# A two-layer decoder on one core: token tile 0's next-stage input made during tile 1's last matmuls, and no modulation sums in a stage's last blocks

## The chip, the core and the metric

One core of a Trainium2 chip runs the whole program in one launch. The metric is the device time of one execution in microseconds (us). Times quoted from a trace are those of one profiled execution, counted from its first instruction.

## The reference

Two decoder layers act on x, 256 tokens of width 2048, float32. Each layer has a token mixer and an MLP, each fed by a modulated input and closed by a LayerNorm:

```
mod = silu(c) @ w_ada[l] + b_ada[l]
sh_a, sc_a, g_a, sh_m, sc_m, g_m = split(mod, 6)
h = x * (1 + sc_a) + sh_a
y = mixer(h)                        # projections, 8 + 8 heads, output projection w_o
x = layernorm(ALPHA * x + (1 + g_a) * y)
h = x * (1 + sc_m) + sh_m
y = square(relu(h @ w_up)) @ w_down  # hidden 8192
x = layernorm(ALPHA * x + (1 + g_m) * y)
```

## The kernel before

The tokens are two tiles of 128. Every weight is read as float32 in **blocks** of 256 rows by 512 columns (two k-tiles of 128 rows, 512 KB, a DMA of line 140 into one of 7 buffers `raw`). ScalarE (ACT) rounds the block to `wh` (line 134), VectorE (DVE) makes the remainder `wl = raw - wh` (line 135), and TensorE (PE) forms each product from three matmuls: hi·wh, hi·wl, lo·wh (lines 302 to 304 for `proj`, token-major; 328 to 331 for `proj_T`; 908 and 910 for the MLP's `up`). `wh` and `wl` have three buffers each, so a block can be split at most three blocks ahead of PE.

The modulation `c @ w_ada` is not done on PE. It is made of **sums** on DVE, one per 512 KB of `w_ada` (line 148, the data loaded by line 156 into the same 7 buffers). Their order is a list `side`: `block()` advances it by a rate per block (`RATES`), and `side_until` advances it at once as far as somebody needs a result. Sixteen sums give one part of the modulation; its accumulator is then transposed on PE (line 166) and reduced on DVE (line 171).

There are four stages: mixer and MLP of layer 0, mixer and MLP of layer 1, so three inner **boundaries**. The mixer ends with the output projection of 4 chunks of 512 columns (8 blocks each); after a chunk `add_gated` multiplies the result by the gate, adds it to `xacc` and takes statistics (lines 496, 497, 499 for each tile). In the last chunk of a stage `proj_tail` holds the last 4 blocks in SBUF (buffers `room`), runs them for token tile 0 and then for token tile 1, and calls `norm_first` on tile 0: statistics, a power on GpSimd (POOL, line 507), four normalizations (line 512). After the tail `norm_h` does the same for tile 1 and `make_h` builds the next stage's input `hT`: transposes on PE (line 471), scale and shift on ACT (line 484), rounding and remainder on DVE (lines 486, 487). The first blocks of the next stage take both tiles at once.

A scheduler in the framework sets the order in which each engine gets its instructions; an engine then runs its own list in that order.

Of the kernel before, what the change touches and what calls it, by code (L numbers as in the profile page):

```python
# [18 lines left out]
P = 128  # L19
# [30 lines left out]
SKIP = 2  # L50
AHEAD = 10
TAIL = (8, 12)
OTAIL = 8
# [7 lines left out]
STEP = ((2, 2), (2, 2))  # L61
RATES = ((0.8, 0.8, 1.0, 0.6, 1.2), (1.1, 0.53, 0.64, 0.25))

# [10 lines left out]
def decoder(ctx: ExitStack, tc: tile.TileContext, x, c, positions, w_ada, b_ada, w_in, b_f,  # L74
# [230 lines left out]

    def proj(po, lhs, wrows, c0, kt0, kt1, first=True, last=True):
# [10 lines left out]
    def proj_T(po, hT, wrows, c0, kt0, kt1, first=True, last=True):  # L317
# [16 lines left out]
    def proj_tail(po, lhs, wrows, c0, kt0, kt1, done):  # L334


        room = big.tile([P, 4, 2, 2, CW], F32R, tag="hT", name="room")
# [175 lines left out]

    def norm_first(stats):

        ms = row_stats(stats, 0)
        for q in range(4):
            normalize(0, q, *ms)

    def norm_h(stats, A, B, coef, key, end=KT):  # L520

        ms = [None] + [row_stats(stats, t) for t in range(1, NT)]
        hT = big.tile([P, KT, 2, S], F32R, tag="hT", name="hT")

        def steps():
            for q in range(4):
                for t in range(1, NT):
                    normalize(t, q, *ms[t])
                yield from make_h(hT, A, B, q * 4, q * 4 + 4, coef)

        h_steps[:] = [steps(), 0, end]
        hold[0] = HOLDS[key]
        need_h(AHEAD)
        return hT
# [220 lines left out]

    def mixer(l, hT, gate_key, stats, passes, done):

# [22 lines left out]
        def chunk(name, kt0=None, kt1=None, hold=False):  # L780
# [6 lines left out]
            if name in ("fq0", "fk0", "fq1", "fk1"):  # L787
                proj_T(po, hT, wr, c0, kt0, kt1, fresh, not hold)
            else:
                proj(po, lhs, wr, c0, kt0, kt1, fresh, not hold)  # L790
            if hold:
# [88 lines left out]
        for chs in ((0, 1), (2,), (3,)):  # L880
            pos = [[mm() for _ in range(NT)] for _ in chs]
            final_ch = chs == (3,)
            for kt0 in (8, 0):
                if kt0 == 0:
# [4 lines left out]
            if final_ch:  # L889
                proj_tail(pos[0], lhs_o, wo, 3 * CW, 8 - OTAIL, 8, lambda t: finish(3, pos[0], t))  # L890
# [4 lines left out]
    def mlp(l, hT, gate_key, stats, done, halves, pieces):  # L895

        wu = rows_of(w_up[l])

        def up(c0, kt0, kt1):
            pu = [mm(), mm(), bank(), bank()]  # L900
            for kb in range(kt0, kt1, 2):
                wh, wl = block(wu(kb, 2, c0, CW), 2, CW)
                need_h(kb + AHEAD)
                for j in range(2):
                    kt = kb + j
                    for f in range(4):
                        cs = slice(f * P, (f + 1) * P)
                        nc.tensor.matmul(pu[f], lhsT=wh[:, j, cs], rhs=hT[:, kt].rearrange("p a s -> p (a s)"),  # L908
                                         start=kt == kt0, stop=False)
# [4 lines left out]
        def up_narrow(c0, kt0, kt1):  # L914

            pu = [mm() for _ in range(2)]
            proj_T(pu, hT, wu, c0, kt0, kt1)
            return [p.rearrange("p (f s) -> p f s", f=2) for p in pu]
# [20 lines left out]
        for g in range(NG):  # L939
            Hs = [big.tile([P, 8, 2, S], F32R, tag="hm", name="Hs", bufs=2) for _ in range(2)]  # L940
            sets = range(GRP // CW)
            if g == 0 and halves is not None:
                for fs in range(LEAD):
                    part = g4([P, 4, S], "part")
                    for i, p in enumerate(up_narrow(fs * CW, 0, 8)):
                        nc.scalar.copy(part[:, 2 * i:2 * i + 2, :], p)
# [43 lines left out]
    def coeffs(l, vec, ln):  # L990
# [59 lines left out]
    for l in range(DEPTH):  # L1050
# [53 lines left out]
```

## Time and profile before

| | |
|---|---|
| median of 3 runs | 2377.34 us (2375.9 to 2378.76) |
| the profiled execution | 2369.32 us |
| its span, first to last instruction | 2367.6 us |
| PE busy | 2281.3 us (96%) |
| DVE busy | 1790.1 us (76%) |
| ACT busy | 1155.3 us (49%) |
| DMA read | 615.07 MB, 261 GB/s over the span |

PE is busy for all but some 86 us of the span, so time can come only from its idle stretches or from its work; DVE's share is an average, near full in the first half of the program and lower in the second.

### The profile page before, as it was taken

What the parts mean: (1) busy time and instruction counts of PE and PEld (TensorE: products, weight loads), DVE (VectorE), ACT (ScalarE), POOL (GpSimd) and SP (SyncE); (2) the same over time, 40 slices, a digit from 0 to 9 for tenths busy, and PEclk for the clock granted to TensorE, in tenths of its full rate; (3) what the DMA queues carried; (4) which work ended last, traced back from release to release, by engine and by line L of the source; (5) the groups of instructions that cost most, each with busy time, mean ns of one, the idle gap of its engine ahead of it and who ended that gap; (6) DMA issues with size and microseconds to landing.
All of it is one profiled execution on the core that took longest, in us unless ns stands there. A gap on an engine that the chain in (4) does not pass through costs nothing.

```text
span 2367.6 us, 33293 instructions
## 1 busy us (share of the span) xinstructions
PE 2281.3 (96%) x12444; PEld 1959.6 (83%) x12444; DVE 1790.1 (76%) x2339; ACT 1155.3 (49%) x1684; POOL 35.1 (1%) x60
## 2 busy tenths in 40 slices
PE   4999999899999999999999999999999999999998
PEld 3878798699989888888777778987888888888886
DVE  7899888988888778888777975667675666555657
ACT  2543675344546345346444663444554553553542
POOL 0000010000000000000000000000000000000000
PEclk9999999999999999999999999999999999999999
DMA  9999688889898888888759877765777777756653
GB/s 344 326 331 308 193 265 305 312 315 325 303 349 301 302 281 309 312 293 300 273 186 303 292 226 234 233 215 170 221 263 251 229 242 240 230 189 195 187 188 123
DMA packets 309890, 619.37 MB, mean 262 GB/s; under 512 B 24200, under 2 KB 25048, under 8 KB 309728
## 3 DMA queue, kind: packets, MB, share of 16 engines
q1 hardware_dynamic: 309728, 617.25, 77.6%
q8 instruction: 97, 1.59, 0.3%
q14 instruction: 65, 0.53, 0.1%
HBM read 615.07 MB, written 2.10 MB: 261 GB/s over the span
## 4 chain that ended last, share of the span: by engine, by line
PE 76%; DVE 9%; DMA 9%; issue 3%; ACT 2%; POOL 0%; SPq 0%; DVEq 0%; ACTq 0%; POOLq 0%
PE mm L303 13%; PE mm L302 13%; PE mm L304 13%; PE mm L908 7%; PE bank L908 7%; DMA rawa<-in_w_ada_dram 5%; PE mm L331 4%; PE mm L330 4%; PE mm L328 4%; PE mm L910 4%; PE bank L910 4%; DVE wl L135 4%; DVE acc L148 2%; DMA raw<-in_w_in_dram 1%; ACT wh L134 1%
## 5 line engine op out<-in xcount | busy, mean ns | idle before, releaser
L134 ACT CAST wh<-raw 128x1024 fp32r<-128x1024 f32 x752 | 789.5, 1052 | 929.5 <-PE mm L304 491.5
L135 DVE TENSOR_TENSOR wl<-raw,wh 128x1024 fp32r<-128x1024 f32 x752 | 913.7, 1221 | 347.2 <-ACT wh L134 343.9
L148 DVE SCALAR_TENSOR_TENSOR acc<-rawa,cact,acc 128x1024 f32<-128x1024 f32 x368 | 471.0, 1280 | 137.8 <-DMA rawa<-in_w_ada_dram 136.5
L303 PE MATMUL mm<-wl,Hs 128*128 128x512 f32 x992 | 386.5, 390 | 2.0 <-DVE wl L135 1.9
L302 PE MATMUL mm<-wh,Hs 128*128 128x512 f32 x992 | 386.2, 389 | 0.0
L304 PE MATMUL mm<-wh,Hs 128*128 128x512 f32 x992 | 386.0, 389 | 0.0
L331 PE MATMUL mm<-hT,wl 128*128 128x256 f32 x1024 | 289.6, 285 | 6.0 <-DVE wl L135 5.4
L328 PE MATMUL mm<-hT,wh 128*128 128x256 f32 x1024 | 290.9, 285 | 1.9 <-DVE hT L486 1.1
L330 PE MATMUL mm<-hT,wh 128*128 128x256 f32 x1024 | 289.8, 284 | 0.2 <-DVE hT L487 0.2
L908 PE MATMUL mm<-hT,wh 128*128 128x512 f32 x768 | 286.7, 396 | 0.5 <-DVE hT L487 0.5
L908 PE MATMUL bank<-hT,wh 128*128 128x512 f32 x768 | 286.2, 395 | 0.0
L303 PEld LDWEIGHTS mm<-wl,Hs 128*128 128x128 f32 x992 | 186.2, 188 | 41.9 <-DVE wl L135 3.5
L302 PEld LDWEIGHTS mm<-wh,Hs 128*128 128x128 f32 x992 | 186.2, 188 | 38.7
L304 PEld LDWEIGHTS mm<-wh,Hs 128*128 128x128 f32 x992 | 186.2, 188 | 38.6
L910 PE MATMUL mm<-hT,wl 128*128 128x256 f32 x768 | 215.5, 281 | 0.2 <-DVE wl L135 0.2
L910 PE MATMUL bank<-hT,wl 128*128 128x256 f32 x768 | 215.3, 280 | 0.0
L302 PE MATMUL mm<-wh,hT 128*128 128x512 f32 x512 | 200.8, 400 | 5.9 <-DVE hT L486 5.7
L303 PE MATMUL mm<-wl,hT 128*128 128x512 f32 x512 | 203.4, 397 | 3.1 <-DVE wl L135 2.7
L331 PEld LDWEIGHTS mm<-hT,wl 128*128 128x128 f32 x1024 | 196.0, 192 | 8.7 <-DVE wl L135 8.3
L304 PE MATMUL mm<-wh,hT 128*128 128x512 f32 x512 | 200.9, 393 | 0.0
L328 PEld LDWEIGHTS mm<-hT,wh 128*128 128x128 f32 x1024 | 196.8, 192 | 3.4 <-DVE hT L486 1.3
L330 PEld LDWEIGHTS mm<-hT,wh 128*128 128x128 f32 x1024 | 197.1, 192 | 0.8 <-DVE hT L487 0.4
(248 smaller groups left out, 2665.7 us busy)
## 6 DMA issues: line engine op xcount, KB each, us to landing
rawa<-in_w_ada_dram SPq DMA_DIRECT2D x384, 512.0 KB, 5.5
raw<-in_w_up_dram SPq DMA_DIRECT2D x256, 512.0 KB, 4.8
raw<-in_w_down_dram SPq DMA_DIRECT2D x256, 512.0 KB, 5.1
raw<-in_w_in_dram SPq DMA_DIRECT2D x192, 512.0 KB, 5.4
raw<-in_w_o_dram SPq DMA_DIRECT2D x64, 512.0 KB, 4.6
gb<-in_ln_g_dram SPq DMA_DIRECT2D x12, 256.0 KB, 5.5
bb<-in_ln_b_dram SPq DMA_DIRECT2D x12, 256.0 KB, 5.3
xacc<-in_x_dram SPq DMA_DIRECT2D x8, 256.0 KB, 6.7
```

Source lines behind the costliest of these rows:

```text
L134: nc.scalar.copy(wh, raw)
L135: nc.vector.tensor_sub(wl, raw, wh.bitcast(F32))
L148: nc.vector.scalar_tensor_tensor(acc, raw, k, acc, ALU.mult, ALU.add)
L302: nc.tensor.matmul(o, lhsT=hi, rhs=wh, start=start, stop=False)
L303: nc.tensor.matmul(o, lhsT=hi, rhs=wl, start=False, stop=False)
L304: nc.tensor.matmul(o, lhsT=lo, rhs=wh, start=False, stop=stop)
L328: nc.tensor.matmul(o, lhsT=wh[:, j, cs], rhs=hT[:, kt, 0, :], start=first and kt == kt0 and f % 2 == 0, stop=False)
L330: nc.tensor.matmul(o, lhsT=wh[:, j, cs], rhs=hT[:, kt, 1, :], start=False, stop=False)
L331: nc.tensor.matmul(o, lhsT=wl[:, j, cs], rhs=hT[:, kt, 0, :], start=False, stop=last and kt == kt1 - 1 and f % 2 == 1)
L908: nc.tensor.matmul(pu[f], lhsT=wh[:, j, cs], rhs=hT[:, kt].rearrange("p a s -> p (a s)"), start=kt == kt0, stop=False)
L910: nc.tensor.matmul(pu[f][:, 0:S], lhsT=wl[:, j, cs], rhs=hT[:, kt, 0, :], start=False, stop=kt == kt1 - 1)
```

## The change

1. **The list of sums.** In the tail's blocks the list is not advanced (`quiet=True`). The rate in layer 0's output projection goes from 1.0 to 1.2 sums a block. Before the last chunk of a stage, `ahead()` calls `side_until` for the modulation that the next stage's input needs; in layer 0's mixer these are the first two of four parts.
2. **Tile 0's input early.** `norm_first` allocates `hT` and, for the first 8 of 16 k-tiles, makes tile 0's part with `h_part`: 8 transposes, 8 activations 128 wide, rounding on ACT, remainder on DVE. `norm_h` does tile 1 in the same way; the other 8 k-tiles go through `make_h` for both tiles.
3. **The next stage's first three blocks** (6 k-tiles) are split together and run for tile 0, then for tile 1 (`lead`). In `proj` (boundary 2) the matmuls stay as they are, in another order. In `proj_T` (boundary 1) 72 matmuls 256 columns wide become 144 of 128 columns. In `up` (boundary 3) 24 of 512 become 48 of 256, and 24 of 256 become 48 of 128.
4. **The tail's buffers.** Two of the tail's four blocks stay in the `wh`/`wl` buffers, two go to a buffer of the tag `hm`, since `hT`'s is now taken.

```diff
-RATES = ((0.8, 0.8, 1.0, 0.6, 1.2), (1.1, 0.53, 0.64, 0.25))
+RATES = ((0.8, 0.8, 1.2, 0.6, 1.2), (1.1, 0.53, 0.64, 0.25))
...
-            ws.append(block(wrows(kb, 2, c0, CW), 2, CW, (room[:, i, 0], room[:, i, 1]) if i < 4 else None))
+            ws.append(block(wrows(kb, 2, c0, CW), 2, CW, into[i], quiet=True))
...
+    def h_part(hT, A, B, t, q):
+        ts = slice(t * P, (t + 1) * P)
+        pt = bank().rearrange("p (a s) -> p a s", a=4)
+        h32 = e2([P, 4, P], "h32")
+        for j in range(4):
+            kt = q * 4 + j
+            nc.tensor.transpose(pt[:, j, :], xacc[:, t, kt * P:(kt + 1) * P], ident)
+            nc.scalar.activation(h32[:, j, :], pt[:, j, :], AF.Identity, bias=B[:, kt:kt + 1], scale=A[:, kt:kt + 1])
+        hi = hT[:, q * 4:q * 4 + 4, 0, ts]
+        if t == 0:
+            nc.scalar.copy(hi, h32)
+        else:
+            nc.vector.tensor_copy(hi, h32)
+        nc.vector.tensor_sub(hT[:, q * 4:q * 4 + 4, 1, ts], h32, hi.bitcast(F32))
...
         for q in range(4):
             normalize(0, q, *ms)
+            if q < 2:
+                h_part(hT, A, B, 0, q)
...
+        if lead:
+            ws = lead_blocks(wrows, c0, kt0)
+            for t in range(NT):
+                for i in range(ONE):
...
+            if final_ch:
+                ahead()
...
+        def coefs_ahead(end=KT):
+            for k0 in range(0, end, 4):
+                cs[2](k0)
```

How this moves the instructions is read from the two programs' lists. First DVE in layer 0's output projection, from a block of the third chunk to the next splits. `L135` (later `L136`) is a split, `L148` (`L149`) a sum, `L496`, `L497`, `L499` (`L532`, `L533`, `L535`) are the third chunk's gate, addition and statistics. Before:

```order
L135 TENSOR_TENSOR wl_4410<-raw_4407,wh_4409 128x1024
L148 SCALAR_TENSOR_TENSOR acc_4313<-rawa_4404,cact_82,acc_4313 128x1024
L135 TENSOR_TENSOR wl_4441<-raw_4438,wh_4440 128x1024
L148 SCALAR_TENSOR_TENSOR acc_4313<-rawa_4435,cact_82,acc_4313 128x1024
L135 TENSOR_TENSOR wl_4462<-raw_4459,wh_4461 128x1024
L496 TENSOR_TENSOR tmp_4425<-mm_4238,gate0_2_1_3814 128x512
L496 TENSOR_TENSOR tmp_4429<-mm_4239,gate0_2_1_3814 128x512
L497 TENSOR_TENSOR xacc_84<-xacc_84,tmp_4425 128x512
L497 TENSOR_TENSOR xacc_84<-xacc_84,tmp_4429 128x512
L499 BN_STATS stats_103<-xacc_84 128x6 x2
L148 SCALAR_TENSOR_TENSOR acc_4313<-rawa_4456,cact_82,acc_4313 128x1024
L135 TENSOR_TENSOR wl_4483<-raw_4480,wh_4482 128x1024
```

Here `wl_4410` is the third chunk's last block, and two blocks of the last chunk (`wl_4441`, `wl_4462`) are split ahead of the third chunk's gate. After (the third chunk's last block is the split just above these rows):

```order
L149 SCALAR_TENSOR_TENSOR acc<-rawa,cact,acc 128x1024 x2
L532 TENSOR_TENSOR tmp<-mm,gate_2_1_3777 128x512
L149 SCALAR_TENSOR_TENSOR acc<-rawa,cact,acc 128x1024
L533 TENSOR_TENSOR xacc<-xacc,tmp 128x512
L532 TENSOR_TENSOR tmp<-mm,gate_2_1_3777 128x512
L535 BN_STATS stats<-xacc 128x6
L533 TENSOR_TENSOR xacc<-xacc,tmp 128x512
L149 SCALAR_TENSOR_TENSOR acc<-rawa,cact,acc 128x1024
L535 BN_STATS stats<-xacc 128x6
L149 SCALAR_TENSOR_TENSOR acc<-rawa,cact,acc 128x1024 x2
L136 TENSOR_TENSOR wl<-raw,wh 128x1024
```

No block of the last chunk is split ahead any more, and four sums stand between the third chunk's gate and the first split. PE at the same place, after (`mm_4264` is the third chunk, `mm_4450` the last one):

```order
L305 MATMUL mm_4264<-wh_4426,MXf_2949 128x512
L167 MATMUL bank_4473<-ident_75,acc_4225 128x128 x4
L167 MATMUL bank_4478<-ident_75,acc_4225 128x128 x4
L303 MATMUL mm_4450<-wh_4498,MXd_2163 128x512
L304 MATMUL mm_4450<-wl_4499,MXd_2163 128x512
```

The 8 transposes of the finished accumulator, which waits for the last of those sums, now stand ahead of the last chunk's first matmul; before they stood behind the tail. Last, DVE at boundary 3 after the change, from tile 0's gate on (`L541` leads to POOL's power, `L548` normalizes, `L564` is the remainder of tile 0's input):

```order
L532 TENSOR_TENSOR tmp<-mm,gate_2_1_11216 128x512
L533 TENSOR_TENSOR xacc<-xacc,tmp 128x512
L535 BN_STATS stats<-xacc 128x6
L539 BN_AGGR mv<-stats 128x2
L541 TENSOR_SCALAR ve<-mv 128x1
L136 TENSOR_TENSOR wl<-raw,wh 128x1024
L548 TENSOR_SCALAR xacc<-xacc,mv,rs 128x512 x4
L136 TENSOR_TENSOR wl<-raw,wh 128x1024
L532 TENSOR_TENSOR tmp<-mm,gate_2_1_11216 128x512
L533 TENSOR_TENSOR xacc<-xacc,tmp 128x512
L535 BN_STATS stats<-xacc 128x6
L564 TENSOR_TENSOR hT<-h_15715,hT 128x4x128
```

Two splits of the next stage's blocks, and tile 1's gate, addition and statistics, stand ahead of tile 0's remainder. Boundary 2 has the same order; boundary 1 has it too, with a sum behind tile 1's gate and another behind its statistics.

## Rows read from the trace of the kernel before

**Rows 1.** PE's waits, whole run: who, for whom, total us, times, longest us.

```profile
PE bank L471 <- DVE xacc L512: 15.0, 4, 6.9
```

**Rows 2.** PE timeline, layer 0's last output chunk: start us, us, instruction, count [idle].

```profile
441.10 0.39 PE L302 MATMUL mm<-wh,MXd 128*128 128x512 f32 x1
441.33 0.39 PE L303 MATMUL mm<-wl,MXd 128*128 128x512 f32 x1
...
446.54 0.61 PE L302 MATMUL mm<-wh,MXd 128*128 128x512 f32 x2
448.86 0.50 PE L303 MATMUL mm<-wl,MXd 128*128 128x512 f32 x1 [1.71 <-DVE wl L135]
```

**Rows 3.** DVE timeline, the same place.

```profile
442.81 1.28 DVE L496 TENSOR_TENSOR tmp<-mm,gate 128x512 f32<-128x512 f32 x2
444.00 1.29 DVE L497 TENSOR_TENSOR xacc<-xacc,tmp 128x512 f32<-128x512 f32 x2
445.21 1.28 DVE L499 BATCH_NORM_STATS2 stats<-xacc 128x6 f32<-128x512 f32 x2
446.40 1.27 DVE L148 SCALAR_TENSOR_TENSOR acc<-rawa,cact,acc 128x1024 f32<-128x1024 f32 x1
447.59 1.22 DVE L135 TENSOR_TENSOR wl<-raw,wh 128x1024 fp32r<-128x1024 f32 x1
448.72 1.28 DVE L148 SCALAR_TENSOR_TENSOR acc<-rawa,cact,acc 128x1024 f32<-128x1024 f32 x1
```

**Rows 4.** PE timeline, boundary 1.

```profile
472.45 0.66 PE L471 MATMUL bank<-ident,xacc 128*128 128x128 f32 x2 [6.86 <-DVE xacc L512]
472.90 1.91 PE L166 MATMUL bank<-ident,acc 128*128 128x128 f32 x8
475.91 3.06 PE L471 MATMUL bank<-ident,xacc 128*128 128x128 f32 x14 [1.10 <-DVE xacc L512]
478.73 0.48 PE L328 MATMUL mm<-hT,wh 128*128 128x256 f32 x2
```

**Rows 5.** DVE timeline, boundary 1.

```profile
462.39 2.60 DVE L148 SCALAR_TENSOR_TENSOR acc<-rawa,cact,acc 128x1024 f32<-128x1024 f32 x2
464.90 1.41 DVE L496 TENSOR_TENSOR tmp<-mm,gate 128x512 f32<-128x512 f32 x2
```

**Rows 6.** DVE timeline, boundary 2, token tile 0.

```profile
1200.28 0.69 DVE L496 TENSOR_TENSOR tmp<-mm,gate 128x512 f32<-128x512 f32 x1 [3.13 <-PE mm L304]
...
1202.46 0.26 DVE L503 BATCH_NORM_AGGREGATE mv<-stats 128x2 f32<-128x24 f32 x1
...
1203.63 1.92 DVE L512 TENSOR_SCALAR xacc<-xacc,mv,rs 128x512 f32<-128x512 f32 x4 [0.72 <-POOL rs L507]
```

**Rows 7.** PE timeline, boundaries 2 and 3.

```profile
1205.53 0.60 PE L471 MATMUL bank<-ident,xacc 128*128 128x128 f32 x4
1209.68 3.33 PE L471 MATMUL bank<-ident,xacc 128*128 128x128 f32 x16 [3.55 <-DVE xacc L512]
...
1641.14 2.31 PE L471 MATMUL bank<-ident,xacc 128*128 128x128 f32 x16 [3.50 <-DVE xacc L512]
```

**Rows 8.** Window at boundary 2: us, busy us (count) by engine, PEclk, DMA.

```profile
1206.00:1212.50 6.50, 2.95 (x15) 2.83 (x14) 4.92 (x11) 1.88 (x5) 0.54 (x1) 0.74 0.01 1
```

**Rows 9.** PE timeline, an attention head between projection matmuls.

```profile
314.47 0.28 PE L331 MATMUL mm<-hT,wl 128*128 128x256 f32 x1
314.59 0.82 PE L622 MATMUL bank<-fk,fq 128*128 128x128 f32 x4
315.06 0.58 PE L626 MATMUL bank<-FR,FL 128*128 128x128 f32 x2
315.47 0.28 PE L328 MATMUL mm<-hT,wh 128*128 128x256 f32 x1
```

**Rows 10.** Window 400 to 447 us, DVE alone: busy us (count), PEclk, DMA share, GB/s.

```profile
400.00:447.00 47.00, 41.69 (x49) 1.00 0.86 297
```

**Rows 11.** DMA issues: count, KB each, us to landing.

```profile
rawa<-in_w_ada_dram SPq DMA_DIRECT2D x384, 512.0 KB, 5.5
```

More of the change, by code (lines that the diff above doesn't have):

```diff
@@ L51 @@
 AHEAD = 10
+ONE = 6
 TAIL = (8, 12)
@@ L304, in mm3, with lead_blocks, proj @@
         nc.tensor.matmul(o, lhsT=lo, rhs=wh, start=False, stop=stop)
-    def proj(po, lhs, wrows, c0, kt0, kt1, first=True, last=True):
+    def lead_blocks(wrows, c0, kt0):
+        return [block(wrows(kb, 2, c0, CW), 2, CW) for kb in range(kt0, kt0 + ONE, 2)]
+    def proj(po, lhs, wrows, c0, kt0, kt1, first=True, last=True, lead=False):
+        if lead:
+            ws = lead_blocks(wrows, c0, kt0)
+            for t in range(NT):
+                for i in range(ONE):
+                    kt = kt0 + i
+                    wh, wl = ws[i // 2]
+                    mm3(po[t], lhs(kt, 0, t), lhs(kt, 1, t), wh[:, i % 2, :], wl[:, i % 2, :],
+                        first and i == 0, last and kt == kt1 - 1)
+            first, kt0 = False, kt0 + ONE
         for kb in range(kt0, kt1, 2):
@@ L315, in proj, with proj_T @@
                         first and kt == kt0, last and kt == kt1 - 1)
-    def proj_T(po, hT, wrows, c0, kt0, kt1, first=True, last=True):
+    def proj_T(po, hT, wrows, c0, kt0, kt1, first=True, last=True, lead=False):
+        if lead:
+            ws = lead_blocks(wrows, c0, kt0)
+            for t in range(NT):
+                ts = slice(t * P, (t + 1) * P)
+                for i in range(ONE):
+                    kt = kt0 + i
+                    wh, wl = ws[i // 2]
+                    for f in range(4):
+                        cs = slice(f * P, (f + 1) * P)
+                        o = po[f // 2][:, (f % 2) * S + t * P:(f % 2) * S + (t + 1) * P]
+                        nc.tensor.matmul(o, lhsT=wh[:, i % 2, cs], rhs=hT[:, kt, 0, ts],
+                                         start=first and i == 0 and t == 0 and f % 2 == 0, stop=False)
+                        nc.tensor.matmul(o, lhsT=wh[:, i % 2, cs], rhs=hT[:, kt, 1, ts], start=False, stop=False)
+                        nc.tensor.matmul(o, lhsT=wl[:, i % 2, cs], rhs=hT[:, kt, 0, ts], start=False, stop=False)
+            first, kt0 = False, kt0 + ONE
         for kb in range(kt0, kt1, 2):
@@ L332, in proj_T, with proj_tail @@
                                      stop=last and kt == kt1 - 1 and f % 2 == 1)
-    def proj_tail(po, lhs, wrows, c0, kt0, kt1, done):
-        room = big.tile([P, 4, 2, 2, CW], F32R, tag="hT", name="room")
+    def proj_tail(po, lhs, wrows, c0, kt0, kt1, done, end):
+        n = (kt1 - kt0) // 2
+        if end:
+            room = big.tile([P, 4, 2, 2, CW], F32R, tag="hT", name="room")
+            into = [(room[:, i, 0], room[:, i, 1]) for i in range(4)] + [None] * (n - 4)
+        else:
+            room = big.tile([P, 2, 2, 2, CW], F32R, tag="hm", name="room", bufs=2)
+            into = [None] * (n - 2) + [(room[:, i, 0], room[:, i, 1]) for i in range(2)]
         ws = []
         for i, kb in enumerate(range(kt0, kt1, 2)):
-            ws.append(block(wrows(kb, 2, c0, CW), 2, CW, (room[:, i, 0], room[:, i, 1]) if i < 4 else None))
+            ws.append(block(wrows(kb, 2, c0, CW), 2, CW, into[i], quiet=True))
         for t in range(NT):
@@ L518, in norm_first @@
             normalize(0, q, *ms)
+            if q < 2:
+                h_part(hT, A, B, 0, q)
+        next_h.append(hT)
+    next_h = []
     def norm_h(stats, A, B, coef, key, end=KT):
[L522 to L523 removed]
+        ms = row_stats(stats, 1)
+        hT = next_h.pop()
         def steps():
             for q in range(4):
[L527 to L529 removed]
+                normalize(1, q, *ms)
+                if q < 2:
+                    h_part(hT, A, B, 1, q)
+                    yield q * 4 + 4
+                else:
+                    yield from make_h(hT, A, B, q * 4, q * 4 + 4, coef)
         h_steps[:] = [steps(), 0, end]
@@ L754, in forget, with mixer @@
         nc.vector.tensor_add(FG[0:R], tA, tB)
-    def mixer(l, hT, gate_key, stats, passes, done):
+    def mixer(l, hT, gate_key, stats, passes, done, ahead):
         wr = rows_of(w_in[l])
@@ L789, in chunk @@
             else:
-                proj(po, lhs, wr, c0, kt0, kt1, fresh, not hold)
+                proj(po, lhs, wr, c0, kt0, kt1, fresh, not hold, l > 0 and name == "dv0")
             if hold:
@@ L893, in mixer, with mlp, up @@
                     add_gated(po, gate_key, ch, stats, True)
-    def mlp(l, hT, gate_key, stats, done, halves, pieces):
+    def mlp(l, hT, gate_key, stats, done, halves, pieces, ahead):
         wu = rows_of(w_up[l])
-        def up(c0, kt0, kt1):
+        def up(c0, lead):
             pu = [mm(), mm(), bank(), bank()]
+            kt0, kt1 = 0, KT
+            if lead:
+                ws = lead_blocks(wu, c0, 0)
+                for t in range(NT):
+                    ts = slice(t * P, (t + 1) * P)
+                    for kt in range(ONE):
+                        wh, wl = ws[kt // 2]
+                        for f in range(4):
+                            cs = slice(f * P, (f + 1) * P)
+                            o = pu[f].rearrange("p (a s) -> p a s", a=2)
+                            nc.tensor.matmul(o[:, :, ts], lhsT=wh[:, kt % 2, cs], rhs=hT[:, kt, :, ts],
+                                             start=kt == 0 and t == 0, stop=False)
+                            nc.tensor.matmul(o[:, 0, ts], lhsT=wl[:, kt % 2, cs], rhs=hT[:, kt, 0, ts],
+                                             start=False, stop=False)
+                kt0 = ONE
             for kb in range(kt0, kt1, 2):
@@ L971, in mlp @@
                 tail = last and ch == 3
+                if tail:
+                    ahead()
                 proj(po, lhs, wd, ch * CW, 0, KT - TAIL[l] if tail else KT, True, not tail)
```

37 lines of the change are left out of this document (24 added, 13 removed).

## The prediction

> **What bounds the kernel now.** PE is busy for 2281.3 of 2367.6 us, so I read first where PE waits. The largest entry that this change can touch is the wait of the boundary transposes for normalized `xacc`: 15.0 us in four waits [rows 1]. Its places are the three inner boundaries: 6.86 and 1.10 us at the first [rows 4], 3.55 at the second and 3.50 at the third [rows 7]. At boundary 1 the reader sees why nothing is hidden: the gate for *both* tiles starts only at 464.90, behind two sums [rows 5], though tile 0's matmuls come first. At boundary 2 the tail works as meant: DVE had been idle 3.13 us when tile 0's gate began, and the four normalizations end 5.3 us later [rows 6], about as long as tile 1's 24 matmuls take (24 x 0.227 = 5.4 us; 0.227 is the distance of two starts in [rows 2]). Then I read layer 0's last output chunk, where the change moves sums: PE waits 1.71 us there for a split, although two blocks had been split ahead [rows 2]. DVE's pieces there: a gate piece 0.60, a sum 1.19, a split 1.13 us from start to start [rows 3].
>
> **The change, part by part.**
>
> *A, layer 0's last output chunk.* `ahead()` puts the rest of a part's sums before the chunk. By the order of the program, two sums run while the third chunk still computes, but four stand behind its gate, which waits for that chunk's matmuls, and PE's next instructions are the transposes of the finished accumulator. So from tile 0's end: 6 gate pieces x 0.60 + 4 sums x 1.19 = 8.4 us, less the 0.7 us in which tile 1's last three matmuls run: PE stands still 7.7 us. The price is safe from below, since every piece was timed, and rows 3 are the same chain with one sum: 3.6 + 1.2 + 1.1 = 5.9 us against 5.4 us of split-ahead work and a wait of 1.71. Then a second wait: after the transposes DVE does two reductions (0.6 each, as a gate piece), three sums (one a first one, cheaper; I take 3.1 together) and a split, 1.2 + 3.1 + 1.1 = 5.4, while PE has 12 matmuls and two more, 3.2: 2.2 us, between 0 (if PE is slow after its idle time) and 3. The sums' data: 512 KB each, 5.5 us to land [rows 11], through the 7 shared buffers; a buffer comes free only when its sum is done, so the third block may come late: 0 to 3, I take 1. The wait of 1.71 goes. A = 7.7 + 2.2 + 1.0 - 1.7 = **+9.2** (6 to 12). The 8 transposes move here from boundary 1.
>
> *E, the rate 1.2.* Four more sums in the first 24 blocks, 4.8 us of DVE. DVE was idle 5.3 of 47 us there [rows 10] and PE had next to no wait, so the splits' lead of one to three blocks covers most: **+0.5** (0 to 4.8). The sums come out of layer 0's MLP, where they wait for nobody: nothing gained.
>
> *B, boundary 1.* Tile 0's chain after its last matmul: 3.35 us to the first normalization [rows 6], plus 0.4 because a split is now put into POOL's 0.72 us, then 0.46 each: first quarter at 4.4, all at 5.8. The transposes stand after 19 of tile 1's matmuls (4.3 us): this fits, a wait of 0.3. But the input is ready only with its remainder, and DVE has ahead of that a split (to 6.9), tile 1's gate, a sum and then the remainder itself (0.6): 9.4 us. PE is through at 6.6: idle 2.8. It then does 21 lead matmuls, and the next row in its list is a transpose of tile 1, whose normalization comes at 14.1 (a second remainder, addition, statistics, a sum, 1.2 us of aggregate and power as in [rows 6], 0.5): idle 2.6. Together 5.7 against 8.0: -2.3. The 24 transposes took 0.66 + 1.91 + 3.06 = 5.6 us [rows 4]; 0.11 each where PE had not stood still (4 in 0.60, the last one's 0.27 included) and 0.2 after it had [rows 7], so 3.6 now: -2.0. The granted clock shows the cause, 0.74 in the window of boundary 2 [rows 8]: part of it at the lower of the two levels, 1.2 GHz. Last, 72 matmuls of 256 columns at 0.12 become 144 of 128. The trace has one 128-wide matmul of this type per attention head: from 314.59 to 315.47 run two records of 128 columns at 0.11 and two of 256 at 0.22 (the older type, twice the time a column, as the transposes), then one of 128 and one of 256 [rows 9]; 0.88 - 0.66 - 0.12 leaves 0.10. Bounds: 0.06 (columns alone) and 0.12 (no gain from fewer columns). 144 x 0.10 - 72 x 0.12 = +5.8 (0 to 8.6). B = -2.3 - 2.0 + 5.8 = **+1.5** (-4.3 to +4.3).
>
> On this price the Trainium skill (TensorE: Matmul & The Clock Gate, Back-to-back issue gap) states a sustained 81 ns for a 128-column matmul with its weight load. By that figure B would be smaller by 2.7 and D below by 0.9 us, an estimate of 2387 us for the whole; no run before this shows a row of such matmuls.
>
> *C, boundary 2.* The same chain without sums: the remainder ends at 9.6 (three gate pieces in place of gate and sum), PE idles 0.3 + 2.6, and 0.7 for tile 1's normalization at 11.9: 3.6 in place of 3.55. The 20 transposes fall from 0.60 + 3.33 [rows 7] to 2.2 if PE keeps its clock: -1.7. No matmul is added. C = **-1.6** (-5.2 if the idle time goes too, +1).
>
> *D, boundary 3.* Idle 0.3 + 3.0 + 1.4 = 4.7 against 3.50: +1.2. The transposes took no longer than a normalization lets them (16 in 2.31), so nothing is taken off there. 24 x (2 x 0.12 - 0.227) + 24 x (2 x 0.10 - 0.12) = +2.2. D = **+3.4** (-1.3 to +5).
>
> *At no cost:* the tail's blocks in `hm` (the buffer is free when the tail begins; DVE has no sums there), and the smaller activations (ACT is busy for 49% of the span).
>
> **Sum:** 9.2 + 0.5 + 1.5 - 1.6 + 3.4 = +13.0. The profiled execution took 2369.3, so 2382.3; it lies 8.0 below the median of the runs, on which the forecast is 2377.3 + 13.0 = **2390 us**. A measurement tells about 0.2%, 4.8 us, from no change.
>
> **The rivals.**
>
> 1. *The sums hide (faster).* If DVE had the burst behind it before the third chunk ends, A would be -1.7, and with less to do DVE would close the boundaries' idle time (8.0, 3.55, 3.50) too: B -4.2, C -5.2, D -1.3, together -12.4: 2365. It needs the four sums ahead of the gate in DVE's list, or a gate that doesn't wait for the chunk; the list has them behind. What speaks for it is that the change takes sums out of [rows 5], where they do cost. 10%.
> 2. *Two halves cancel (no change).* A as above, but tile 0's remainder is ready when PE gets through the tail, 6.6 us after tile 0 and not 9.4, and tile 1's when the lead ends: 9.2 + 0.5 - 4.2 - 5.2 - 1.3 = -1.0: 2376. For it: [rows 6] show DVE idle 3 us before tile 0's gate. Against: two splits and tile 1's gate stand ahead of the remainder. It decides at 3 us of that chain. 14%.
> 3. *The transfers bind (slower still).* Around the burst ten transfers of 512 KB come in a row; at the 297 GB/s of [rows 10], 1.77 us each, 17.7 against some 11 us of DVE work: +7: 2397. Against: these 297 are what the sums asked for, with the engines at 0.86. 12%.
>
> The forecast itself has 64%. That the change doesn't do what it says holds in part already: tile 0's input is begun, not finished, during tile 1's matmuls.
>
> **How the numbers follow.** Rival 1 and the luckiest ends of the forecast make faster 0.11; rival 2 and the forecast's low end 0.14 for the same; the rest, 0.75, is slower. The forecast's own bounds together would reach from about -6 to +27; they don't fall on one side all at once, and half of each spread gives 2383 to 2399. To leave out no more than 2 in 10 the range takes in rivals 2 and 3: 2376 to 2402.
>
> **What would show it.** In the profile after: one PE wait of 7 to 8.5 us at the transposes of the accumulator (line 167) just before layer 0's last output chunk, and a second of about 2 us for a split in its second block; at each boundary two shorter waits in place of one, the first ended by the remainder (line 564), the second by tile 1's normalization (line 548); 128-wide lead matmuls 0.10 us apart in boundary 1. Wrong would be: no wait at line 167 (rival 1), boundaries with under 2 us of idle time in all (rival 2), or sums that wait for DMA in that chunk (rival 3).

## The result, and the profile after

The changed kernel takes **2410.44 us** (median of 4 runs, 2406.44 to 2410.84) against 2376.62 for the kernel before on the same chip: ratio 1.0147, 95% interval 1.0117 to 1.0176. Slower was forecast, but by 13.0 us (2390, range 2376 to 2402); it is 33.8. The profiled execution took 2410.84, its span is 2409.1, so the two profiles stand 41.5 us apart: that of the kernel before was one of its quick executions (2369.32).

The page of the changed kernel: the span, PE's row of section 1, and PE's granted clock in 40 slices of 60 us.

```profile
span 2409.1 us, 33568 instructions
PE 2318.5 (96%) x12564; PEld 1989.5 (83%) x12564; DVE 1790.7 (74%) x2333; ACT 1166.9 (48%) x1714; POOL 35.9 (1%) x60
PEclk9999999879999999999999999999999999999999
```

PE is *busy* 37.2 us longer than before, with the same products to form, while its idle time grew by 4.3 us (86.3 to 90.6). So most of the loss is not in waits, where the prediction looked for it, but in matmuls that were more in number or ran slower: the clock's row has an 8 and a 7 in slices 8 and 9 (422 to 542 us). To see where, I took in both traces the time at which PE had streamed the same number of columns, transposes left out:

| place | before | after | later by | step of the prediction | forecast |
|---|---|---|---|---|---|
| output projection of layer 0, second chunk | 411.6 | 411.4 | -0.3 | | |
| its third chunk | 437.5 | 442.1 | 4.6 | E: +4.9 | +0.5 |
| its tail | 462.9 | 477.5 | 14.6 | A: +10.0 | +9.2 |
| MLP of layer 0, behind the lead | 500.8 | 532.9 | 32.1 | **B: +17.5** | +1.5 |
| the same MLP, in its tail | 1198.9 | 1233.2 | 34.3 | (none): +2.2 | 0 |
| mixer of layer 1, behind the lead | 1243.3 | 1278.3 | 34.9 | C: +0.7 | -1.6 |
| its output projection | 1617.5 | 1653.0 | 35.5 | (none): +0.6 | 0 |
| MLP of layer 1 | 1915.9 | 1957.3 | 41.5 | D: +6.0 | +3.4 |

**Boundary 1.** PE's timeline in the changed kernel. `L344`, `L346`, `L347` are the lead's narrow matmuls (128 columns), `L557` the transposes of `h_part`, `L357` the first matmuls of 256 columns.

```profile
484.23 0.44 PE L344 MATMUL mm<-hT,wh 128*128 128x128 f32 x2 [1.05 <-ACT hT L561]
...
486.80 0.27 PE L344 MATMUL mm<-hT,wh 128*128 128x128 f32 x1
486.91 0.28 PE L346 MATMUL mm<-hT,wh 128*128 128x128 f32 x1
489.75 0.45 PE L557 MATMUL bank<-ident,xacc 128*128 128x128 f32 x1 [2.56 <-DVE xacc L548]
...
517.84 0.41 PE L346 MATMUL mm<-hT,wh 128*128 128x128 f32 x1
518.05 0.41 PE L347 MATMUL mm<-hT,wl 128*128 128x128 f32 x1
518.27 0.52 PE L357 MATMUL mm<-hT,wh 128*128 128x256 f32 x1
...
521.15 0.41 PE L359 MATMUL mm<-hT,wh 128*128 128x256 f32 x1
...
521.65 0.28 PE L359 MATMUL mm<-hT,wh 128*128 128x256 f32 x1
```

And stretches of 4 us there (columns as in [rows 8]: busy time and count by engine, then the granted clock, the DMA share, GB/s).

```profile
484.00:488.00 4.00, 2.66 (x20) 2.38 (x20) 3.75 (x6) 0.70 (x2) 0.00 (x0) 0.92 0.63 217
488.00:492.00 4.00, 2.25 (x11) 1.93 (x11) 3.30 (x8) 1.56 (x4) 0.55 (x1) 0.50 0.40 131
...
512.00:516.00 4.00, 4.00 (x21) 4.00 (x20) 1.89 (x2) 1.04 (x1) 0.00 (x0) 0.50 0.29 103
```

The first 20 narrow matmuls are 0.11 us apart (486.80 to 486.91), the other 124, once the transposes are through, 0.21 (517.84 to 518.05). From 488 on the granted clock is 0.50, which is 1.2 GHz, and it stays there although PE does not stand still once after 489.75. It rises at about 521.5, behind the first matmuls of 256 columns. Before, at this place, the clock was 1.00 again at about 478.6, as the first product began (478.73 [rows 4]), with nothing but transposes run since the wait.

**Layer 0's output projection.** PE's timeline:

```profile
425.34 0.50 PE L304 MATMUL mm<-wl,MXd 128*128 128x512 f32 x1 [2.93 <-DVE wl L136]
...
427.19 0.63 PE L304 MATMUL mm<-wl,MXd 128*128 128x512 f32 x1
427.62 0.63 PE L305 MATMUL mm<-wh,MXd 128*128 128x512 f32 x1
...
453.93 1.94 PE L167 MATMUL bank<-ident,acc 128*128 128x128 f32 x8 [8.09 <-DVE acc L149]
...
461.26 0.50 PE L304 MATMUL mm<-wl,MXd 128*128 128x512 f32 x1 [0.19 <-DVE wl L136]
```

The burst (A) shows as forecast: 8.09 us at the accumulator's transposes, behind the sums. In place of the second wait of about 2 us (0.19 here) PE's matmuls behind the burst run at 0.43 in place of 0.227, so the term came out right with another composition. E is new: a wait of 2.93 us at the second chunk's gate, and 0.43 a matmul for some 3 us behind it. DVE's timeline tells why a split is late there:

```profile
416.07 0.69 DVE L172 TENSOR_REDUCE red<-bank 128x4 f32<-128x512 f32 x1 [0.85 <-PE bank L167]
...
418.02 1.28 DVE L149 SCALAR_TENSOR_TENSOR acc<-rawa,cact,acc 128x1024 f32<-128x1024 f32 x1
419.21 1.28 DVE L532 TENSOR_TENSOR tmp<-mm,gate 128x512 f32<-128x512 f32 x2
...
422.87 1.28 DVE L149 SCALAR_TENSOR_TENSOR acc<-rawa,cact,acc 128x1024 f32<-128x1024 f32 x1
424.06 1.22 DVE L136 TENSOR_TENSOR wl<-raw,wh 128x1024 fp32r<-128x1024 f32 x1
```

With 1.2 sums a block a part of the modulation ends at 416 instead of 427; its reductions, three sums (the first of a part is a short one, 0.74 us) and the gate then come in one row, and no split begins between 414.00 and 424.06.

**Boundary 3.** Windows of the changed kernel: its two long waits were 1.78 and 0.87 us, and between them the clock falls here too (before it was 1.00 throughout).

```profile
1676.00:1680.00 4.00, 1.62 (x11) 1.36 (x11) 3.17 (x7) 1.25 (x3) 0.55 (x1) 0.82 0.37 114
1680.00:1684.00 4.00, 4.00 (x21) 3.83 (x20) 1.00 (x3) 3.15 (x8) 0.00 (x0) 0.50 0.00 0
```

### The profile page after: what moved, and what is told of

It reads as the page before. It is cut to its first block, busy times and chain, and to the rows that moved or that the text cites. A ratio compares the mean times of both kernels' runs of the same rounds, so it can differ in the third digit from the quotient of the medians.

```text
span 2409.1 us, 33568 instructions
## 1 busy us (share of the span) xinstructions
PE 2318.5 (96%) x12564; PEld 1989.5 (83%) x12564; DVE 1790.7 (74%) x2333; ACT 1166.9 (48%) x1714; POOL 35.9 (1%) x60
## 3 DMA queue, kind: packets, MB, share of 16 engines
q8 instruction: 98, 1.61, 0.3%
## 5 line engine op out<-in xcount | busy, mean ns | idle before, releaser
L135 ACT CAST wh<-raw 128x1024 fp32r<-128x1024 f32 x758 | 795.1, 1050 | 990.7 <-PE mm L305 506.9
L136 DVE TENSOR_TENSOR wl<-raw,wh 128x1024 fp32r<-128x1024 f32 x758 | 921.6, 1222 | 369.3 <-ACT wh L135 365.1
L149 DVE SCALAR_TENSOR_TENSOR acc<-rawa,cact,acc 128x1024 f32<-128x1024 f32 x368 | 471.2, 1280 | 142.2 <-DMA rawa<-in_w_ada_dram 140.6
L360 PE MATMUL mm<-hT,wl 128*128 128x256 f32 x1000 | 283.2, 286 | 5.4 <-DVE wl L136 5.1
L357 PE MATMUL mm<-hT,wh 128*128 128x256 f32 x1000 | 284.9, 286 | 1.9 <-DVE hT L522 1.1
L359 PE MATMUL mm<-hT,wh 128*128 128x256 f32 x1000 | 283.6, 284 | 0.2 <-DVE hT L523 0.2
L988 PE MATMUL mm<-hT,wl 128*128 128x256 f32 x756 | 211.8, 280 | 0.0
L357 PEld LDWEIGHTS mm<-hT,wh 128*128 128x128 f32 x1000 | 193.1, 193 | 3.4 <-ACT wh L135 1.3
L359 PEld LDWEIGHTS mm<-hT,wh 128*128 128x128 f32 x1000 | 193.0, 193 | 0.6 <-DVE hT L523 0.4
```

Of the source, the lines that this page charges most:

```text
L135: nc.scalar.copy(wh, raw)
L136: nc.vector.tensor_sub(wl, raw, wh.bitcast(F32))
L149: nc.vector.scalar_tensor_tensor(acc, raw, k, acc, ALU.mult, ALU.add)
```

## The experiments

Twelve kernels ran, beside the kernel before on the same chip (its medians there: 2372.3 to 2374.3).

### The narrow matmuls and the clock

`e1_b1_wide`, no lead at boundary 1:

```diff
-                    for i, p in enumerate(up_narrow(fs * CW, 0, 8, fs == 0)):
+                    for i, p in enumerate(up_narrow(fs * CW, 0, 8)):
```

> The changed kernel, but boundary 1 has no lead: the first blocks take both tiles, 72 matmuls of 256 columns in place of 144 of 128. Theory (narrow matmuls keep the clock at its lower level, 0.50, after the wait of 2.56 us has let it fall): first matmul at about 492, half clock for a few us only, the 72 done by about 505 in place of 518.3: 2397 us (2394 to 2400). Rival (after such a wait the clock stays low for some 32 us whatever runs): granted clock 0.50 until about 521 also here, 2406 us.

Measured: 2398.31 us, ratio to before 1.0102 (1.0078 to 1.0126). PE now waits 6.56 us in one piece for tile 1 and its first product starts at 492.0, where the theory had put it. Then, in its windows:

```profile
492.00:496.00 4.00, 3.72 (x15) 3.42 (x16) 1.85 (x4) 0.00 (x0) 0.00 (x0) 0.50 0.52 171
496.00:500.00 4.00, 4.00 (x30) 4.00 (x29) 2.07 (x2) 1.05 (x1) 0.00 (x0) 0.79 0.46 120
```

The wait was longer than the changed kernel's, yet the clock is back at about 497.6, not 521: so it is not a fixed time at the lower level. At this boundary e1 gains 13.9 us.

`e2_narrow_mid`, the kernel before with 192 narrow matmuls where PE is in full work (`ts` is a token tile's 128 columns):

```diff
-                    for i, p in enumerate(up_narrow(fs * CW, 0, 8)):
+                    for i, p in enumerate(up_narrow(fs * CW, 0, 8, fs == 4)):
...
+                    if narrow:
+                        for t in range(NT):
...
+                            nc.tensor.matmul(o, lhsT=wh[:, j, cs], rhs=hT[:, kt, 0, ts],
```

> The kernel before, with 96 matmuls of 256 columns in the middle of the MLP's first blocks (column set 4, four blocks) made into 192 of 128 columns; PE does not wait ahead of them. Theory (narrow matmuls only hold a clock that has fallen): 0.112 us each at clock 1.00, 192 x 0.112 - 96 x 0.12 = +10: 2387 us. Rival (narrow matmuls lower the clock by themselves): 0.213 us each, +29: 2406 us.

Measured: 2394.76 us (1.0095, 1.0069 to 1.0122). Its windows while the narrow ones run (about 524 to 546 us):

```profile
528.00:536.00 8.00, 8.00 (x75) 8.00 (x73) 1.23 (x1) 1.97 (x2) 0.00 (x0) 1.00 0.58 204
536.00:544.00 8.00, 8.00 (x75) 8.00 (x74) 4.21 (x6) 1.17 (x2) 0.00 (x0) 1.00 0.31 81
```

The clock stays 1.00 and they are 0.111 us apart: here the narrow matmuls did not lower the clock, and up to their end the trace is 9.0 us behind the kernel before, as the theory said. The other 12 us come later, most of it as waits for splits (2.94 us from 552.8 on, 3.45 from 666.4 on, and smaller ones); that part of the expectation was wrong.

`e3_b1_two`, a lead of one block at boundary 1:

```diff
-            ws = lead_blocks(wrows, c0, kt0)
+            ws = lead_blocks(wrows, c0, kt0, 2)
...
-                for i in range(ONE):
+                for i in range(2):
```

> The changed kernel with a lead of one block (2 k-tiles) instead of three at boundary 1: 48 narrow matmuls instead of 144. Theory (narrow matmuls hold the clock): half clock lasts until a few us after the 48th, near 499, the same work done at about 504 in place of 518.3: 2396 us. Rival (a fixed time): clock low until about 521, 2406 us.

Measured: 2398.65 us (1.0113, 1.0092 to 1.0134). PE's timeline:

```profile
500.61 0.41 PE L347 MATMUL mm<-hT,wl 128*128 128x128 f32 x1
500.83 0.52 PE L357 MATMUL mm<-hT,wh 128*128 128x256 f32 x1
...
503.49 0.41 PE L357 MATMUL mm<-hT,wh 128*128 128x256 f32 x1
...
503.88 0.28 PE L360 MATMUL mm<-hT,wl 128*128 128x256 f32 x1
```

The first wide matmul starts at 500.83, and at about 503.8 the clock is at 1.00 again; in the changed kernel, with three times as many narrow ones, the two times are 518.27 and 521.5. The end of the low stretch moves with the last narrow matmul.

`f6_fill_after`, the changed kernel with its whole narrow lead, and 14 wide matmuls whose result nobody reads:

```diff
+                    if t == 0 and i == 0:
+                        pf = bank()
+                        for n in range(FILL):
+                            nc.tensor.matmul(pf, lhsT=ones_r, rhs=wh[:, 0, :], start=n == 0, stop=n == FILL - 1)
```

> The changed kernel with all 144 narrow matmuls at boundary 1, and 14 matmuls of 512 columns of no use among tile 1's first transposes, behind the wait of 2.56 us. Theory (narrow matmuls hold a fallen clock, wide ones bring it back): the 14 take about 4.5 us, the clock is 1.00 some 4 us after the wait, the rest of the narrow ones take 0.112 in place of 0.213 (126 x 0.10 = 12.7 less): -8, 2402 us. Rival (it is not the width that holds the clock): the 14 come on top, 2415 us.

Measured: 2405.93 us (1.0134, 1.0108 to 1.0160). PE's timeline (`L352` is the filler):

```profile
489.79 0.41 PE L348 MATMUL mm<-hT,wl 128*128 128x128 f32 x1
490.00 0.41 PE L345 MATMUL mm<-hT,wh 128*128 128x128 f32 x1
...
492.43 1.20 PE L352 MATMUL bank<-wh,ones_r 128*128 128x512 f32 x2
...
498.41 0.28 PE L345 MATMUL mm<-hT,wh 128*128 128x128 f32 x1
498.52 0.28 PE L347 MATMUL mm<-hT,wh 128*128 128x128 f32 x1
```

Ahead of the filler the narrow matmuls are 0.21 apart, behind it 0.11, and the clock is 1.00 until the lead's end. So with wide matmuls among them (f6), or in their place (e1, e3), the clock came back, and with the narrow ones alone it did not: they are what held it down here. The number of columns alone does not tell why. These are windows of the kernel before, at boundaries 1 and 2:

```profile
476.00:480.00 4.00, 4.00 (x23) 3.85 (x24) 3.60 (x11) 1.93 (x4) 0.00 (x0) 0.67 0.40 128
1212.00:1216.00 4.00, 4.00 (x24) 3.43 (x22) 3.86 (x9) 3.42 (x9) 0.00 (x0) 0.94 0.00 0
```

By these means the clock rose at about 478.6 and 1212.5, ahead of the first products (478.73 [rows 4] and 1212.76), when PE had run nothing since its waits but transposes, which are 128 columns wide too (in the older type, 0.21 us apart at 0.50). What sets the narrow products apart from these was not tested.

In time the filler earned less than the 8 us expected: 4.5 us between the medians, 2.2 when each kernel is set against its own kernel before (31.6 and 33.8), which the intervals do not tell apart. A wait of 4.15 us for a split follows from 518.0 on, since PE reached the next block sooner than DVE.

### The sums

`e6_b1_old` and `e8_sums_only` take the change apart: the first has layer 0's projection and boundary 1 as before and the early input at boundaries 2 and 3; the second has the list of sums and the tail's buffers of the changed kernel and no early input or lead.

```diff
 e6_b1_old
-RATES = ((0.8, 0.8, 1.2, 0.6, 1.2),
+RATES = ((0.8, 0.8, 1.0, 0.6, 1.2),
...
-            if final_ch:
+            if final_ch and l > 0:
                 ahead()
...
-        hT = norm_h(stats, *cs, 8 if early_up else KT)
+        hT = (norm_h_old if l == 0 else norm_h)(stats, *cs, 8 if early_up else KT)
...
 e8_sums_only
...
-        hT = norm_h(stats, *cs, 8 if early_up else KT)
+        hT = norm_h_old(stats, *cs, 8 if early_up else KT)
...
```

> The early half, without the sums of layer 0's mixer: layer 0's output projection and boundary 1 as in the kernel before (rate 1.0, no ahead(), sums in the tail, both tiles together); boundaries 2 and 3 as in the changed kernel. Theory (E, A and boundary 1 hold nearly all of the loss; boundary 3 costs 6.0, boundary 2 0.7): 2374 + 6.7 = 2381 us (2378 to 2384). Rival (boundaries 2 and 3 lose only because the sums ahead of them are late): 2374 us.

> The other half: the list of sums and the tail's buffers as in the changed kernel, no early input for tile 0 and no lead at any boundary. Theory (the sums of layer 0's output projection are paid where they stand): E +4.85 and A +10.0, some 2 of waits in layer 0's MLP, less about 4.5 at boundary 1, whose idle time falls from 8.0 to about 3.5: 2374 + 12.4 = 2386 us (2383 to 2390). Rival (the sums cost nothing by themselves, the early input does): 2374 us.

Measured: e6 2377.70 us, +5.4 (1.0020, 1.0008 to 1.0033); e8 2390.36, +18.0 (1.0079, 1.0058 to 1.0100). No part is free. e6 is near its theory (+6.7); e8 lies 5.6 above its own (+12.4), by about what boundaries 2 and 3 cost in its trace (2.9 and 2.6), for which the theory had nothing. The parts can't simply be added: these 5.5 us lie where e6 has its +5.4 too, and neither kernel has the early input at boundary 1 with wide matmuls, where by the columns streamed e1 loses 3.6 us and e8 gains 3.3. That 18.0 + 5.4 and the 9.4 by which e1 lies nearer to its kernel before (33.8 - 24.4) make 32.8, almost the whole 33.8, is in part chance. PE's waits of e8 at boundaries 2 and 3:

```profile
1225.68 0.69 PE L507 MATMUL bank<-ident,xacc 128*128 128x128 f32 x2 [5.29 <-DVE xacc L548]
...
1660.15 3.68 PE L507 MATMUL bank<-ident,xacc 128*128 128x128 f32 x16 [5.24 <-DVE xacc L548]
```

There the input is made as before, but PE waits 5.3 and 5.2 us in place of 3.55 and 3.50 [rows 7]. DVE's timeline at boundary 2 of e8 has two splits of the next stage inside the chain that [rows 6] shows without them (e8 has the new list of sums and the new buffers, so which of the two puts them there was not tested apart):

```profile
1217.10 1.23 DVE L136 TENSOR_TENSOR wl<-raw,wh 128x1024 fp32r<-128x1024 f32 x1
1218.76 1.92 DVE L548 TENSOR_SCALAR xacc<-xacc,mv,rs 128x512 f32<-128x512 f32 x4 [0.43 <-POOL rs L543]
1220.59 1.22 DVE L136 TENSOR_TENSOR wl<-raw,wh 128x1024 fp32r<-128x1024 f32 x1
```

`e4_ahead_late` calls `ahead()` before the last chunk's tail, so that four blocks are split ahead of the burst:

```diff
-            if final_ch:
-                ahead()
             for kt0 in (8, 0):
...
             if final_ch:
+                ahead()
                 proj_tail(pos[0], lhs_o, wo, 3 * CW, 8 - OTAIL, 8, lambda t: finish(3, pos[0], t), False)
```

> The changed kernel, but ahead() is called before the last chunk's tail, not before its first four blocks, so splits of these stand ahead of the third chunk's gate in DVE's list. Theory (the order of the burst makes the wait): the 8.09 us at line 167 and the slow matmuls behind it go, about 2 us of waits come for splits: 2402 us (2400 to 2405). Rival (DVE's work or the transfers there are the bound): the wait moves to the splits, 2408 or more.

Measured: 2408.80 us (1.0152, 1.0133 to 1.0170). At its place the theory was right. The wait of 8.09 is gone, and this is what is left of it in PE's timeline:

```profile
449.18 0.50 PE L304 MATMUL mm<-wl,MXd 128*128 128x512 f32 x1 [2.33 <-DVE wl L136]
```

By the columns streamed e4 is 2.2 us ahead of the changed kernel before this place and 10.5 behind it. But 7 us are lost again in layer 0's MLP, with waits of 1.15 us at 756 (for ACT's rounding) and 2.50 at 795 (for a split) and a clock of 0.79 in 796 to 804. The time is the rival's.

`f2_late_wide` is e4 with e1's edit, to see whether this comes back by chance:

```diff
-            if final_ch:
-                ahead()
             for kt0 in (8, 0):
...
             if final_ch:
+                ahead()
                 proj_tail(pos[0], lhs_o, wo, 3 * CW, 8 - OTAIL, 8, lambda t: finish(3, pos[0], t), False)
...
-                    for i, p in enumerate(up_narrow(fs * CW, 0, 8, fs == 0)):
+                    for i, p in enumerate(up_narrow(fs * CW, 0, 8)):
```

> e1_b1_wide and e4_ahead_late together: no lead at boundary 1, and ahead() only before the tail. Theory (the burst's order costs 8 us, and what e4_ahead_late lost again in layer 0's MLP was its own chance of waits): 2390 us. Rival (sums held back come back as waits in the MLP whatever the boundary does): 2397 us.

Measured: 2393.61 us (1.0090, 1.0061 to 1.0119), between the two. Waits of 1.15, 1.40 and 2.17 us stand at the same part of the MLP (741 to 781). Open: why the MLP answers to the sums in this way.

`e5_rate_back` is e1 with the rate 1.0, `f3_rate_alone` the kernel before with nothing but the rate 1.2:

```diff
 e5_rate_back
-RATES = ((0.8, 0.8, 1.2, 0.6, 1.2),
+RATES = ((0.8, 0.8, 1.0, 0.6, 1.2),
 f3_rate_alone
-RATES = ((0.8, 0.8, 1.0, 0.6, 1.2),
+RATES = ((0.8, 0.8, 1.2, 0.6, 1.2),
```

> Beside e1_b1_wide (no lead at boundary 1): the rate in layer 0's output projection is 1.0 again, ahead() stays. Theory (the sums are only moved): the 4.85 us at the second chunk's gate go, and four more sums of 1.19 us stand in the burst before the last chunk: 2398 us, no change (2395 to 2400). Rival (the rate is what costs, the burst has cover for more): 2393 us.

> The kernel before with nothing but the rate of layer 0's output projection at 1.2. Theory (the rate makes E by itself: a part's sums end earlier, and their reductions and the next sum push a split behind the second chunk's gate): a wait of about 2.9 us at 421 and half clock behind it, +4.85, less up to 3 at boundary 1, where up to four sums fewer are left: 2375 us (2374 to 2378). Rival (E comes with ahead()): 2370 us.

Measured: e5 2404.41 us (1.0140, 1.0116 to 1.0165), 6.1 *worse* than e1 (7.7 when each is set against its own kernel before); f3 2385.91 (1.0058, 1.0039 to 1.0077), 11.6 worse than before. First the timelines of e5, of PE, of ACT and of the queue that issues the transfers (SPq), then PE's of f3:

```profile
456.40 1.22 PE L303 MATMUL mm<-wh,MXd 128*128 128x512 f32 x2 [14.58 <-ACT wh L135]
...
455.31 1.04 ACT L135 CAST wh<-raw 128x1024 fp32r<-128x1024 f32 x1 [20.44 <-DMA raw<-in_w_o_dram]
...
431.03 17.52 SPq L157 DMA_DIRECT2D rawa<-in_w_ada_dram  x12
449.50 0.37 SPq L141 DMA_DIRECT2D raw<-in_w_o_dram  x1
```

```profile
424.98 0.80 PE L303 MATMUL mm<-wl,MXd 128*128 128x512 f32 x1 [2.96 <-DVE wl L135]
...
479.60 0.66 PE L471 MATMUL bank<-ident,xacc 128*128 128x128 f32 x2 [5.79 <-DVE xacc L512]
```

In e5 the wait at the second chunk is gone, and PE stands still for 14.58 us before the last chunk in place of 8.09. This wait no longer ends with the sums: ACT waits for the data of the chunk's first block, whose transfer is issued at 449.50, behind the data of twelve sums. So the burst has a second price, the transfers of [rows 11] through the shared buffers. By the columns streamed, the two places together cost 16.3 us in e5 and 14.1 in e1; most of the rest of the difference is in layer 0's MLP, where e5 loses 10.9 and e1 3.1. In f3 the wait of 2.96 us is there without `ahead()`: the rate makes E by itself (+6.1 at this place). The rest of f3's expectation was wrong: boundary 1 gives nothing back (5.79 and 2.75 us in place of 6.86 and 1.10 [rows 4]), and the MLP has new waits.

### Boundary 3, and a filler in the waits

`e7_b13_wide` is e1 without a lead at boundary 3:

```diff
-                up_out(up(c0, c0 == 0) if early is None else up_narrow(c0, 8, KT), Hs, fs, early)
+                up_out(up(c0, False) if early is None else up_narrow(c0, 8, KT), Hs, fs, early)
```

> Beside e1_b1_wide: boundary 3 without lead too, so no matmul is narrower than before anywhere. Theory (the narrower matmuls, at half clock for 5 us, make most of boundary 3's loss of 6.0): 4 us less than e1_b1_wide, 2394 us. Rival (the lead hides tile 1's chain, and without it PE waits as much longer): 2398 us.

Measured: 2397.01 us (1.0100, 1.0079 to 1.0122), no change that can be told from e1. PE's timeline:

```profile
1666.08 0.91 PE L557 MATMUL bank<-ident,xacc 128*128 128x128 f32 x2 [4.05 <-DVE xacc L548]
...
1671.87 0.79 PE L986 MATMUL mm<-hT,wh 128*128 128x512 f32 x1 [1.61 <-DVE hT L564]
```

Without the lead PE waits 4.05 and 1.61 us; the boundary costs 8.2 in place of 6.0. So the rival holds here: the lead pays for its narrower matmuls at boundary 3, and does not pay enough.

`f5_fill` is the kernel before with a filler in the waits of boundaries 1 and 2 (26 and 12 matmuls):

```diff
+FILL = {(0, 3): 26, (1, 0): 12}
...
+        if key in FILL:
+            pf = bank()
+            for i in range(FILL[key]):
+                nc.tensor.matmul(pf, lhsT=ones_r, rhs=fill_src[0], start=i == 0, stop=i == FILL[key] - 1)
```

> The kernel before, with matmuls of no use in PE's list where it waits for the normalization: 26 of 512 columns at boundary 1 (5.9 us in the wait of 6.86), 12 at boundary 2 (2.7 us in that of 3.55); their result is read by nobody. Theory (a wait costs its length and then a stretch at half clock): the clock stays 1.00, the transposes fall from 5.6 to about 3.6 us and from 3.3 to 2.2, -3 us: 2369 us. Rival (the transposes wait for the normalizations, not for the clock): no change, 2372 us.

Measured: **2369.91 us**, ratio 0.9985 (0.9974 to 0.9997): faster than both kernels, by little. PE's timeline at boundary 1, and a window:

```profile
469.64 6.23 PE L529 MATMUL bank<-room,ones_r 128*128 128x512 f32 x26
476.67 0.41 PE L474 MATMUL bank<-ident,xacc 128*128 128x128 f32 x2 [0.80 <-DVE xacc L515]
476.92 1.04 PE L167 MATMUL bank<-ident,acc 128*128 128x128 f32 x8
```

```profile
476.00:480.00 4.00, 2.39 (x18) 1.99 (x19) 3.93 (x10) 0.19 (x1) 0.56 (x1) 1.00 0.67 231
```

The 8 accumulator transposes take 1.04 us in place of 1.91 [rows 4] at a clock of 1.00 (before, 0.50 to 0.67 between 472 and 480). The wait for DVE is as long as it was; the slow stretch behind it is gone. But new waits for DVE stand in part where it was (0.66 and 0.29 us at the transposes), as the rival said: by the columns streamed boundary 1 is 0.5 us shorter in this trace and boundary 2 0.9. Of the 4.4 us between the medians the boundaries show these 1.4; where the rest comes from is open.

## Why the prediction was wrong

- **A, the burst: right.** 8.09 us at the transposes against 7.7, +10.0 against +9.2. The second wait did not come, because PE was at half clock behind the first; that bound was in the text ("between 0 (if PE is slow after its idle time) and 3"), and the slow matmuls took its place in the sum: that the total came out so near is in part luck. e4 shows that the order of the list makes the wait.
- **E, the rate: mis-sized,** +4.9 against +0.5, just past its upper end of 4.8. The step that failed in it is "the splits' lead of one to three blocks covers most": it took the sums as spread over 24 blocks, where they bring a part's end with its reductions up against a chunk's gate. f3 shows that the rate alone does it.
- **B, boundary 1: the step that made the prediction wrong,** +17.5 against +1.5 and outside its +4.3. The waits were about right: 0.65, 0.21, 0.20, 1.05, 0.29 and 2.56, together 5.0 against 5.7. What failed is "144 x 0.10 - 72 x 0.12 = +5.8" with the bound of 0.12 above. The price of a narrow matmul was read from a head's, which runs at 1.00 [rows 9]. At 1.00 it is 0.11 (20 of them); 124 ran at 0.50 and took 0.21: 124 x 0.10 = 12.4 us more, and some 15 of 256 columns behind them, at 0.21 in place of 0.12, another 1.4. [Rows 8] had the low clock in view, and the text used it for the transposes alone; it did not ask what would bring the clock back. On this price the Trainium skill's figure (TensorE: Matmul & The Clock Gate, Back-to-back issue gap) of 81 ns would have made the forecast smaller; e2 and f6 measure 0.111 to 0.112 at the full clock for this type.
- **C, boundary 2:** +0.7 against -1.6, within its range: the wait fell, to 0.64 and 1.05 us and pieces of 0.2, but the first products of the next stage ran at 0.43 a matmul for some 2 us.
- **D, boundary 3:** +6.0 against +3.4, past +5. The narrower matmuls cost what was said (a pair of 256 and 128 columns 0.23 us, 48 x 0.23 - 24 x (0.227 + 0.12) = +2.7 against +2.2), and the idle time is no more than before; the rest is a clock of 0.50 in 1680 to 1684, which no term had.
- **"At no cost: the tail's blocks in `hm`": not borne out.** In e8, without early input, boundaries 2 and 3 are 2.9 and 2.6 us longer, behind splits that now stand in the chain. That the buffers put them there, and not the list of sums, is not shown. The early input takes part of it back (C is +0.7 in all), and it is not enough.
- **The rivals.** The sums did not hide, and the two halves did not cancel. The third rival (2397, the transfers bind) was nearest in time, by another cause: in the changed kernel the waits at this place end with DVE's sums and splits. But the transfers are close behind: ACT had the last chunk's first block rounded only at 450.70, 4.9 us into the wait of 8.09, and in e5 they end the wait. Rival 2's sign for it, under 2 us of idle time at the boundaries, is not met either.
- **The range.** The terms' own bounds add up to -4.8 and +27.1 (the text has -6), and half of each spread gives 2381 to 2397 and not 2383 to 2399. The range was set by rivals 2 and 3 and does not depend on it.
- Not covered by any step: 2.2 us in layer 0's MLP, where PE waits for splits (0.74, 1.36 and 1.00 us at 578 to 608, against 0.8 in small pieces before). e4, f2, f3 and e5 have more of it at 740 to 800. Its cause stays open.

## What to carry to other kernels

Price a wait of PE as its length plus the stretch at half clock that can follow it, and look at what runs in that stretch: here the clock came back behind matmuls of 256 or 512 columns, or behind transposes, and not once in 124 narrow matmuls. Splitting a matmul by tokens to start earlier costs least where PE comes in at full clock, and it is not free there either (0.111 us for 128 columns, 0.12 for 256). A burst of work on the engine that feeds PE belongs behind as many prepared blocks as the buffers hold, with their data ahead of its own in the queue (in e4 this was worth 8.3 us at its place, most of them lost again later), and when a list of side work is moved, find out on which gates its ends now fall.

## What the runs showed of the chip

- Matmuls of 128 columns back to back ran for 22 us at a granted clock of 1.00 (e2), and for 28 us at 0.50 (the changed kernel, the first 4 us with transposes between), PE never idle in either: in neither stretch did the clock change. It rose while wide ones ran, of 256 columns (the changed kernel, e1, e3) or of 512 (f6), and in the kernel before behind transposes of 128 columns (478.6, 1212.5). The Trainium skill (TensorE: Matmul & The Clock Gate, What's actually happening) says that the way back to the full clock is a matter of time, for narrow matmuls as for wide ones; here it was not, and the measurement decides.
- At 0.50 a matmul of 128 columns takes as long as one of 256, 0.21 us from start to start (e3: 500.61 to 500.83, and 501.15 to 501.36).
- What exactly lowers the clock was not separated. In the changed kernel it fell at about 487.4 (a mean of 0.92 from 484 to 488), 0.2 us after the wait of 2.56 us had begun, so that wait is hardly its cause, though the expectation of e1 took it for that; in f6 and e3 it fell at about 486.3 and 486.7, while narrow matmuls ran behind transposes and waits of 0.2 to 1.05 us.
- Matmuls whose result nobody reads, put into waits that are known to come, kept the clock at 1.00 there (f5). The whole was 0.15% faster (0.03 to 0.26), and the trace places 1.4 us of that at the two boundaries.
